# A two-layer diffusion transformer on one core: the conv border's weight parts, the place of modulation units, PSUM banks, one head's scaling and the last weight block

## The chip, the cores and the metric

The kernel runs on one core of a Trainium2 chip. The metric is the device time of one execution in microseconds (us), the median over runs. TensorE (PE) multiplies, VectorE (DVE), ScalarE (ACT) and GpSimd (POOL) work element by element, and SyncE (SP) issues the transfers from HBM. Each engine executes its own list of instructions in order and waits on semaphores for the others.

## The reference

The program computes two layers (D = 1024) on 256 latent and 256 context tokens, all in fp32. Layer 0 mixes with a short convolution, layer 1 with grouped-query attention over 8 heads. Both have a gated FFN (2816 hidden) before and after the mixer, and each of these three sub-blocks is normalised, modulated by vectors that depend on the condition, and gated:

```python
mod = (silu(c) @ mod_w[i] + mod_b[i]).reshape(bsz, 3, 3, 1, D_MODEL)
lat = lat + 0.5 * mod[:, 0, 2] * swiglu(modulate(lat, norm_g[i, 0], mod[:, 0, 0], mod[:, 0, 1]), w13[i, 0], w2[i, 0])
h = modulate(lat, norm_g[i, 1], mod[:, 1, 0], mod[:, 1, 1])
y = short_conv_mixer(h, ...)        # layer 0;  gqa_mixer(h, hc, ...) in layer 1
lat = lat + mod[:, 1, 2] * y
lat = lat + 0.5 * mod[:, 2, 2] * swiglu(modulate(lat, norm_g[i, 2], mod[:, 2, 0], mod[:, 2, 1]), w13[i, 1], w2[i, 1])
# modulate(t, g, shift, scale) = rms(t) * g * (1 + scale) + shift
```

The context goes the same way (with its own modulation) up to where layer 1's attention has read its keys and values. The result is the latent part.

## The kernel before, in words

**Precision.** [...] Every operand is split in a high part (`wh`, `hh`, ...: ScalarE copies) and a low part (`wl`, `hl`, ...: VectorE subtracts), and a product is three matmuls (`mm3`, L137 to L140), in some stages two. So each block of weights needs a transfer, a copy on ScalarE (1.0 us for 1024 columns) and a subtraction on VectorE (1.2 us) before TensorE can use it.

**Weights.** SP issues all weight transfers in one queue, into `wr` (two buffers of 1 MB); the split parts lie in `wh` and `wl`, four buffers of 1024 columns each. A matmul that is done with a part frees it for the next.

**Modulation.** The vectors `mod` are computed on VectorE by 224 *modulation units* (`mod_unit`, L157, output `junk`): each multiplies 128 rows of the transposed modulation weights with the condition and sums them. Their raw data comes through `wm` (two buffers of 512 KB, `mod_raw`), a transfer serving one or two units. Units are spread over the program by `tick(n)`: it adds n to an account, and for each whole 1 in it puts the next unit at this point of VectorE's order.

**Stages and borders.** The residual `x` is held as eight blocks of 128 columns. Between two stages stands a border: the last two blocks of a projection are finished (`fin`), squared, summed by small matmuls with a column of ones (`ss`, L256), the inverse root is spread over the rows (L276), and the scaled residual (`hr`, by `scaled`) is multiplied and split into the next stage's operands. `open_border` writes this order out by hand. `late(i, s)` are matmuls of the last two blocks that are kept back to give TensorE work meanwhile; `bd.nk` counts the blocks of the projection's inner dimension. With 8 of them the border is *short*: this is only the case from the conv mixer to layer 0's second FFN. `whi(i)` and `wlo(i)` split the first weight halves of the new stage; `ready()` is a square root of one column of the sum so far, on ScalarE.

**FFN.** `border_ffn` follows `open_border` into an FFN: three blocks (`pg`, `pu`) are multiplied plainly, and while that runs the operands and the first weights (`pr`) for block *pairs* are prepared: `Pair` multiplies 2 x 2 blocks with seven products in place of eight, from sums and differences of the weights that VectorE makes (`sub`, L762 to L769, `wr<-wr`; split parts at L744 and L747). From there `ffn` goes over the pairs, each of some 9.9 us, with `tick(PER_PAIR)`, 0.7 of a unit, in each.

**Attention.** PSUM banks are given out in pools by `use_banks`. Per head: `scores` (`psc`), `most` (maxima), `exps`, `weigh` (reciprocal of the sums, then `e` scaled in two halves of 512 on GpSimd, L1661), `turn` (transposes, `pt`, L1672), split, and `mix`.

**Last stage.** The last FFN's second product goes over the residual blocks m = 0 to 7. `w_last` fetches weights for two blocks at a time: two transfers `w2l` of 2048 columns, and `w2m` of 1536 columns, of which each block of the two uses 768, all through `wr`.

Inside borders, pairs and attention the order is the written one; elsewhere a scheduler orders by its own costs.

Of the kernel before, what the change touches and what calls it, by code (L numbers as in the profile page):

```python
# [16 lines left out]
P = 128  # L17
# [8 lines left out]
HEADS = 8  # L26
# [15 lines left out]
def hybrid_kernel(ctx: ExitStack, tc: tile.TileContext, a: dict, out: bass.AP):  # L42
# [29 lines left out]
    def psum(s="ps"):  # L72
        return banks["psm"].tile([P, T2], F32, tag="mm", name=nm(s))
# [36 lines left out]
    def mod_raw():  # L110
        return wp.tile([P, D], F32, name=nm("wm"), tag="wm", bufs=2)
# [5 lines left out]
    def half():  # L117

        return tuple(
            wp.tile([P, 1024], F32R, name=nm(t), tag=t, bufs=4) for t in ("wh", "wl")  # L120
        )
# [71 lines left out]
    def tick(n, behind=None):  # L193

        owed[0] += n
        while (jobs or units) and owed[0] >= 1:
            owed[0] -= 1
            if behind is None:
                next_unit()
            else:  # L200
                with tc.issue_after(behind.ins):
                    next_unit()
# [327 lines left out]
    def open_border(bd, v, early=False):  # L530


        short = bd.nk == KT
        mid = 5 if short else 6

        def whi(i):
            v[i][0].hi(v[i][1])

        def wlo(i):
            v[i][0].lo(v[i][1])  # L540

        ready()
        for s in range(2):
            for k in (4, 5):
                bd.scaled(k, s)
        bd.late(0, 0)
        if short:
            for i in range(2):
                whi(i)
                wlo(i)  # L550
        tick(2)
        bd.fin(0, 0)
        bd.square(0, 0)
        bd.late(0, 1)
        if not short:
            tick(1)
        bd.add(0)
        bd.fin(1, 0)
        bd.square(1, 0)
        bd.late(1, 0, range(mid))  # L560
        if not short:
            whi(0)
        bd.sums(0)
        bd.root(0)
        bd.late(1, 0, range(mid, bd.nk))
        bd.inv(0)
        bd.rows(0)
        if not short:
            wlo(0)
            whi(1)  # L570
        bd.fin(0, 1)
        bd.late(1, 1)
        bd.mult(0, 0)
        bd.square(0, 1)
        bd.hi(low, 0)
        if not short:
            wlo(1)
        bd.add(1)
        bd.mult(1, 0)
        if early:  # L580
            whi(2)
        bd.fin(1, 1)
        bd.hi((4, 5), 0)
        bd.square(1, 1)
        bd.hi((6, 7), 0)
        bd.lo(low, 0)
        return whi, wlo
# [17 lines left out]
    def ready():  # L605

        t = const.tile([P, 1], F32, name=nm("ready"), tag="ready")
        nc.scalar.activation(out=t, in_=accs[0][:, :1], func=AF.Sqrt)
# [216 lines left out]
    def border_ffn(l, b, h, bd):  # L825


        w = [Halves(a["w13"][l, b, i]) for i in range(2)]
        whi, wlo = open_border(bd, [(w[i], j) for i in range(2) for j in range(2)])
        w.append(Halves(a["w13"][l, b, 2]))  # L830
        gs = [new_pair("g") for _ in range(2)]
        pp = [(psum("pg"), psum("pu")) for _ in range(2)]
        post = [Post(p) for p in pp]
        for i in range(2):
            post[i].four(gs[i])

        def groups(i, s):
            return [
                (pp[i][j][:, s * S : s * S + S], lambda k, j=j: w[i]((1 - j) * 1024 + k * P))
                for j in range(2)  # L840
            ]

        def whole(i, s):
            for n in range(3):
                part_mm(groups(i, s), range(KT), n, s, h, True, True)

        g = groups(0, 0)
        for n in range(2):
            part_mm(g, low, n, 0, h, True, False)
        whi(2)  # L850
        bd.sums(1)
        bd.root(1)
        part_mm(g, low, 2, 0, h, False, False)
        bd.lo(high, 0)
        bd.inv(1)
        for n in range(2):
            part_mm(g, high, n, 0, h, False, False)
        whi(3)
        bd.rows(1)
        part_mm(g, high, 2, 0, h, False, True)  # L860
        wlo(2)
        wlo(3)
        pr = Pair(a["w13"][l, b, 3], h)
        bd.shift(low, 0)
        bd.mult(0, 1)
        bd.mult(1, 1)
        bd.shift(high, 0)
        whole(1, 0)
        bd.hi(low, 1)
        bd.lo(low, 1)  # L870
        bd.hi(high, 1)
        bd.lo(high, 1)
        whole(0, 1)
        bd.shift(low, 1)
        tick(1)
        bd.shift(high, 1)
        h.sub(0)
        h.hi("T1")
        h.sub(1)
        h.sub(2)  # L880
        h.lo("T1")
        h.hi("T2")
        post[0].silu()
        h.lo("T2")
        post[0].gate()
        whole(1, 1)
        for i in range(2):
            w[2].hi(i)
            w[2].lo(i)
        post[0].gh()  # L890
        h.sub(3)
        post[0].gl()
        h.hi("T3")
        h.lo("T3")
        pr.hi("A")
        post[1].silu()
        pr.hi("A22")
        pr.lo("A")
        post[1].gate()
        pr.lo("A22")  # L900
        post[1].gh()
        pr.sub(0)
        pr.sub(1)
        pr.hi("S12")
        pr.sub(2)
        post[1].gl()
        pp.append((psum("pg"), psum("pu")))
        for s in range(2):
            g = groups(2, s)
            for n in range(3):  # L910
                part_mm(g, low, n, s, h, s == 0, False)
        for k in high:
            for ps, at in ((pp[2][j], lambda k, j=j: w[2]((1 - j) * 1024 + k * P)) for j in range(2)):
                mm3(ps, at(k), pick(h, k, 0, T2), False, k == KT - 1, True)
        return gs, pr, Post(pp[2])

    def ffn(l, b, h, gate, norm, gs=(), ev=1.5, bd=None):
# [3 lines left out]
        for t in range(2):  # L921
            between = ()
            with tc.manual_schedule(engines=set(QUEUES[:3])) if bd else nullcontext():
# [29 lines left out]
                with nullcontext() if bd else tc.manual_schedule(engines=set(QUEUES[:3])):  # L953
                    for i in range(i1, n):
                        pr, nxt = pair(i), pair(i + 1)
                        if i > i1:
                            pr.lo("S12")
                            pr.lo("S34")
                        elif bd:
                            pr.lo("S12")  # L960
                            pr.hi("S34")
                            pr.lo("S34")
                        pair(i + 2)
                        ask_ahead()
                        if prev:
                            prev.silu()
                        pr.head()
                        if done:
                            done.gate()
                        if nxt:  # L970
                            nxt.both("A22")
                            nxt.sub(0)
                        if done:
                            done.gate_parts()
                        if bd and i == i1:
                            h.hi("T4")
                            h.lo("T4")
                        pr.five()
                        if prev:
                            tick(PER_PAIR)  # L980
                            prev.seven()
                        if nxt:
                            nxt.both("A")
                            nxt.sub(1)
                            nxt.sub(2)
                        pr.six()
                        if nxt:
                            nxt.hi("S12")
                            nxt.hi("S34")
                        if prev:  # L990
                            gs.append(new_pair("g"))
                            prev.four(gs[-1])
                        done, prev = prev, pr
# [661 lines left out]
    def weigh(hd):  # L1655
        e, sm = es[hd]
        r = ap.tile([P, 2], F32, name=nm("r"), tag="r", bufs=3)
        nc.vector.reciprocal(r, sm)
        for qt in range(2):
            c = slice(qt * T2, qt * T2 + T2)  # L1660
            nc.gpsimd.tensor_scalar(  # L1661
                out=e[:, c], in0=e[:, c], scalar1=r[:, qt : qt + 1], scalar2=None, op0=ALU.mult
            )

# [34 lines left out]
    with tc.manual_schedule(engines=set(QUEUES)):  # L1699
# [21 lines left out]
        lo_of(*wvc[1])  # L1721
        sq3 = squares(pq[3])
        g3 = gained(pq[3], qg, 2)
        use_banks(("psc", 2), ("ptp", 2), ("pav", 2))
        scores(0)
        scores(1)
        kc2 = by_cos(*g2)
# [285 lines left out]
    def w_last(m):  # L2013
        if m // 2 not in box:
            t = m // 2
            box[t] = (
                load_w(a["w2l"][t, 0]), load_w(a["w2l"][t, 1]), load_w(a["w2m"][t], 12 * P)
            )
        o = m % 2
        return lambda k: box[m // 2][o](k * P) if k < 16 else box[m // 2][2]((o * 6 + k - 16) * P)  # L2020

    for m in range(KT):
        w = w_last(m)
# [81 lines left out]
```

## Time and profile before

| | us |
|---|---|
| median of 3 runs (lowest to highest) | 1577.05 (1576.33 to 1577.66) |
| the profiled execution | 1575.96 |
| its span in the trace | 1573.9 |
| TensorE busy | 1557.0 (99%) |
| VectorE busy | 1286.5 (82%) |
| ScalarE busy | 755.2 (48%) |
| GpSimd busy | 34.2 (2%) |

Times in the trace count from the start of its span. Where the text says "chain of waits", it is the chain of work followed back from the last instruction, each step to what released it. In windows, the columns are the stretch, its length, the busy time of TensorE, its weight loads, VectorE, ScalarE and GpSimd (with numbers of instructions), the granted TensorE clock (1.00 is full), the busy share of the DMA engines and GB/s. The borders spoken of lie at 550 to 570 us (short, conv to FFN) and 913 us (layer 0 to layer 1); the first pairs behind them start at 613 and 963; attention's scores start at 1314, its head 7 is turned at 1353; the last stage runs from 1506.

### The profile page before, as it was taken

How to read it: one execution, taken by the hardware profiler on the slowest of the kernel's cores; microseconds unless marked ns; L12 is line 12 of the kernel's file. 1: busy time of each engine (PE TensorE's matmuls, PEld its weight loads, DVE VectorE, ACT ScalarE, POOL GpSimd, SP SyncE). 2: the span in 40 equal slices, each digit the busy share in tenths (PEclk: the TensorE clock that was granted, in tenths of full speed). 3: DMA queues.
4: the chain of work that ended last, by engine and by line, in shares of the span. 5: the costliest groups of instructions: out<-in, count | busy, mean ns of one | idle time of the engine just before them, and what ended most of it. 6: DMA issues, size and time to landing. Idle time of an engine off the chain costs nothing.

```text
span 1573.9 us, 25256 instructions
## 1 busy us (share of the span) xinstructions
PE 1557.0 (99%) x10240; PEld 1422.7 (90%) x10240; DVE 1286.5 (82%) x1905; ACT 755.2 (48%) x1261; POOL 34.2 (2%) x28
## 2 busy tenths in 40 slices
PE   9999999999999989999999999999999999999998
PEld 7789899989888889998999899988999899998887
DVE  5788879996999578996999878997998776776654
ACT  4524245535322365532554475532554465775542
POOL 0000000000000000000000000000000002320000
PEclk9999999999999999999999999999999999999999
DMA  9363633363566412355334523357335632345553
GB/s 360 131 209 130 205 111 131 105 212 132 196 214 199 136 67 99 130 188 162 120 122 146 202 95 121 126 197 240 125 131 194 211 124 87 108 161 193 192 176 136
DMA packets 51747, 248.75 MB, mean 158 GB/s; under 512 B 6704, under 2 KB 9264, under 8 KB 36400
## 3 DMA queue, kind: packets, MB, share of 16 engines
q1 hardware_dynamic: 50912, 246.98, 46.1%
q8 instruction: 80, 1.31, 0.3%
q14 instruction: 35, 0.29, 0.1%
q10 hardware_dynamic: 720, 0.17, 0.0%
HBM read 244.77 MB, written 1.05 MB: 156 GB/s over the span
## 4 chain that ended last, share of the span: by engine, by line
PE 94%; DVE 2%; ACT 1%; DMA 1%; issue 0%; POOL 0%; ACTq 0%; DVEq 0%; POOLq 0%
PE py L138 9%; PE py L140 9%; PE py L139 9%; PE p L138 6%; PE p L140 6%; PE p L139 6%; PE q L140 5%; PE q L138 4%; PE q L139 4%; PE pu L1817 3%; PE pg L1817 3%; PE py L1817 2%; PE pg L522 2%; PE pu L522 2%; PE pg L1202 1%; PE pv L138 1%
## 5 line engine op out<-in xcount | busy, mean ns | idle before, releaser
L114 ACT ACTIVATE wh<-wr 128x1024 fp32r<-128x1024 f32 (+1 forms) x210 | 190.7, 926 | 248.4 <-PE py L139 128.1
L157 DVE CUSTOM_DVE_ANT_0 junk<-wm,scbc,modb 128x1024 bf16<-128x1024 f32 x224 | 286.9, 1281 | 24.6 <-DMA wm<-in_modT 22.7
L115 DVE TENSOR_TENSOR wl<-wr,wh 128x1024 fp32r<-128x1024 f32 (+1 forms) x210 | 220.1, 1060 | 71.8 <-ACT wh L114 29.7
L138 PE MATMUL py<-gh,wh 128*128 128x512 f32 (+1 forms) x594 | 217.8, 367 | 0.0
L139 PE MATMUL py<-gl,wh 128*128 128x512 f32 (+1 forms) x594 | 217.3, 366 | 0.0
L140 PE MATMUL py<-gh,wl 128*128 128x512 f32 (+1 forms) x594 | 217.1, 365 | 0.0
L747 DVE TENSOR_TENSOR wl<-wr,wh 128x1024 fp32r<-128x1024 f32 x156 | 186.1, 1218 | 27.7 <-ACT wh L744 27.7
L744 ACT ACTIVATE wh<-wr 128x1024 fp32r<-128x1024 f32 x156 | 160.5, 1056 | 100.5 <-DVE wr L767 59.0
L140 PEld LDWEIGHTS py<-gh,wl 128*128 128x128 f32 x594 | 112.1, 189 | 17.9
L138 PEld LDWEIGHTS py<-gh,wh 128*128 128x128 f32 x594 | 112.1, 189 | 17.7
L139 PEld LDWEIGHTS py<-gl,wh 128*128 128x128 f32 x594 | 112.1, 189 | 17.6
L140 PE MATMUL p<-th,wl 128*128 128x256 f32 x416 | 117.7, 283 | 0.0
L139 PE MATMUL p<-tl,wh 128*128 128x256 f32 x416 | 117.7, 283 | 0.0
L138 PE MATMUL p<-th,wh 128*128 128x256 f32 x416 | 117.7, 283 | 0.0
L138 PE MATMUL q<-bh,wh 128*128 128x256 f32 x304 | 86.0, 283 | 0.0
L139 PE MATMUL q<-bl,wh 128*128 128x256 f32 x304 | 86.0, 283 | 0.0
L140 PE MATMUL q<-bh,wl 128*128 128x256 f32 x304 | 86.0, 283 | 0.0
L139 PEld LDWEIGHTS p<-tl,wh 128*128 128x128 f32 x416 | 79.8, 192 | 0.2
L138 PEld LDWEIGHTS p<-th,wh 128*128 128x128 f32 x416 | 79.8, 192 | 0.2
L140 PEld LDWEIGHTS p<-th,wl 128*128 128x128 f32 x416 | 79.8, 192 | 0.0
L762 DVE TENSOR_TENSOR wr<-wr 128x1024 f32<-128x1024 f32 x52 | 63.7, 1225 | 1.6
L114 ACT ACTIVATE gh<-gm 128x512 fp32r<-128x512 f32 x60 | 37.8, 631 | 52.1 <-DVE gm L820 47.7
(372 smaller groups left out, 4098.1 us busy)
## 6 DMA issues: line engine op xcount, KB each, us to landing
wr<-in_w SPq DMA_DIRECT2D x85, 1024.0 KB, 4.8
wm<-in_modT SPq DMA_DIRECT2D x128, 512.0 KB, 4.2
wr<-in_w2h SPq DMA_DIRECT2D x48, 704.0 KB, 5.3
mr<-in_mod SPq DMA_DIRECT2D x16, 512.0 KB, 8.5
wr<-in_cw_cx SPq DMA_DIRECT2D x8, 1024.0 KB, 4.8
wr<-in_w2l SPq DMA_DIRECT2D x8, 1024.0 KB, 4.9
wr<-in_cw_b SPq DMA_DIRECT2D x4, 1024.0 KB, 5.2
wr<-in_cw_out SPq DMA_DIRECT2D x4, 1024.0 KB, 5.7
```

The costliest lines, as they stand in the source:

```text
L114: nc.scalar.activation(out=hi, in_=src, func=AF.Copy)
L115: nc.vector.tensor_tensor(out=lo, in0=src, in1=hi.bitcast(F32), op=ALU.subtract)
L138: nc.tensor.matmul(ps, wh, mh, start=first, stop=False, **kw)
L139: nc.tensor.matmul(ps, wh, ml, start=False, stop=False, **kw)
L140: nc.tensor.matmul(ps, wl, mh, start=False, stop=last, **kw)
L157: nc.vector.tensor_tensor_reduce(out=junk, in0=raw, in1=scbc[:, v, :], scale=1.0, scalar=modb[:, l, col : col + 1], op0=ALU.mult, op1=ALU.add,
L522: nc.tensor.matmul(ps, w[n == 1], hl if n == 2 else hh, start=first and n == 0 and k == ks[0] and (first is True or g == 0), stop=last and ...
L744: nc.scalar.activation(out=self.shaped(g, 0), in_=self.part(g), func=AF.Copy)
L747: nc.vector.tensor_tensor(out=self.shaped(g, 1), in0=self.part(g), in1=self.shaped(g, 0).bitcast(F32), op=ALU.subtract,)
L762: tt(out=by_two(raw[:, :1024]), in0=a21.unsqueeze(1).to_broadcast([P, 2, T2]), in1=by_two(raw)[:, :, :T2], op=ALU.subtract,)
L1202: nc.tensor.matmul(pps[i][j], w[j][n == 1], hl if n == 2 else hh, start=k == 0 and n == 0, stop=k == KT - 1 and n == 2,)
L1817: nc.tensor.matmul(p[:, :n], w(j, k)[part], m(k)[:, :n], start=not part and k == 0, stop=part == 1 and k == nk - 1, skip_group_check=True,)
```

## The change

Five edits:

1. In the short border the first two weight halves are split (`whi`, `wlo`) ahead of `ready()` in place of behind the scaled residual, and of the two units there one goes behind `fin(1, 0)`.
2. In `border_ffn` two units are put behind `post[1].gl()`; the first pair behind a border gets none (0.7 before).
3. For attention the pools are placed in another order: transposes and outputs get the banks that scores had, scores the last four.
4. Head 7's `e` is scaled by VectorE in place of GpSimd.
5. `w_last` fetches `w2m` as two transfers of 768 columns through the `wm` buffers, each with a split of its own.

```diff
@@ open_border
+        if short:
+            for i in range(2):
+                whi(i)
+                wlo(i)
         ready()
         for s in range(2):
             for k in (4, 5):
                 bd.scaled(k, s)
         bd.late(0, 0)
-        if short:
-            for i in range(2):
-                whi(i)
-                wlo(i)
-        tick(2)
+        tick(1 if short else 2)
         bd.fin(0, 0)
...
         bd.fin(1, 0)
+        if short:
+            tick(1)
         bd.square(1, 0)
@@ border_ffn
         post[1].gl()
+        tick(2)
@@ ffn
                         if prev:
-                            tick(PER_PAIR)
+                            tick(0 if bd and i == i1 else PER_PAIR)
                             prev.seven()
@@ weigh
-            nc.gpsimd.tensor_scalar(
+            eng = nc.vector if hd == HEADS - 1 else nc.gpsimd
+            eng.tensor_scalar(
                 out=e[:, c], in0=e[:, c], scalar1=r[:, qt : qt + 1], scalar2=None, op0=ALU.mult
             )
@@ attention
-        use_banks(("psc", 2), ("ptp", 2), ("pav", 2))
+        use_banks(("ptp", 2), ("pav", 2), ("psc", 2))
@@ w_last
-            box[t] = (
-                load_w(a["w2l"][t, 0]), load_w(a["w2l"][t, 1]), load_w(a["w2m"][t], 12 * P)
-            )
+            ws = [load_w(a["w2l"][t, j]) for j in range(2)]
+            for j in range(2):
+                raw = mod_raw()[:, : 6 * P]
+                nc.sync.dma_start(raw, a["w2m"][t][:, j * 6 * P : (j + 1) * 6 * P])
+                ws.append(tuple(u[:, : 6 * P] for u in half()))
+                split(*ws[-1], raw)
+            box[t] = ws
```

ScalarE in the short border, before (`sq_5068` and `sq_5129` are the squares of residual blocks 4 and 5, `wr_5134` the new stage's first weights):

```order
346 L244 ACTIVATE sq_5068<-x 128x512
347 L244 ACTIVATE sq_5129<-x 128x512
348 L608 ACTIVATE ready_5138<-acc_4938 128x1
349 L412 ACTIVATE hr_5081<-x,A_5077 128x256 x2
350 L412 ACTIVATE hr_5083<-x,A_5077 128x256 x2
351 L498 ACTIVATE wh_5169<-wr_5134 128x1024
352 L498 ACTIVATE wh_5173<-wr_5134 128x1024
353 L437 ACTIVATE sq_5184<-x 128x256
```

And now:

```order
346 L244 ACTIVATE sq_5068<-x 128x512
347 L498 ACTIVATE wh_5138<-wr_5134 128x1024
348 L498 ACTIVATE wh_5142<-wr_5134 128x1024
349 L244 ACTIVATE sq_5129<-x 128x512
350 L610 ACTIVATE ready_5146<-acc_4938 128x1
351 L412 ACTIVATE hr_5081<-x,A_5077 128x256 x2
352 L412 ACTIVATE hr_5083<-x,A_5077 128x256 x2
353 L437 ACTIVATE sq_5180<-x 128x256
```

The two `wh` moved not only ahead of `ready` and `hr`, but ahead of the last whole square too.

VectorE at the same place, before (`py_5102` is block 5 of the projection, `py_5144` and `py_5187` are the late blocks 6 and 7 of the first half of the tokens):

```order
673 L594 TENSOR_SCALAR x<-py_5102,mod_5_3329,x 128x256 x2
674 L247 TENSOR_TENSOR acc_4938<-acc_4938,sq_5129 128x512
675 L503 TENSOR_TENSOR wl_5170<-wr_5134,wh_5169 128x1024
676 L503 TENSOR_TENSOR wl_5174<-wr_5134,wh_5173 128x1024
677 L157 ISA junk_5177,mod_0_4956<-wm_5039,scbc,modb 128x1024
678 L157 ISA mod_0_4956 128x1
679 L157 ISA junk_5179,mod_0_4956<-wm_5039,scbc,modb 128x1024
680 L157 ISA mod_0_4956 128x1
681 L429 TENSOR_SCALAR x<-py_5144,mod_5_3329,x 128x256
682 L442 TENSOR_TENSOR acc_4938<-acc_4938,sq_5184 128x256
683 L429 TENSOR_SCALAR x<-py_5187,mod_5_3329,x 128x256
```

And now:

```order
673 L503 TENSOR_TENSOR wl_5139<-wr_5134,wh_5138 128x1024
674 L596 TENSOR_SCALAR x<-py_5102,mod_5_3329,x 128x256 x2
675 L503 TENSOR_TENSOR wl_5143<-wr_5134,wh_5142 128x1024
676 L247 TENSOR_TENSOR acc_4938<-acc_4938,sq_5129 128x512
677 L157 ISA junk_5177,mod_0_4956<-wm_5039,scbc,modb 128x1024
678 L157 ISA mod_0_4956 128x1
679 L429 TENSOR_SCALAR x<-py_5152,mod_5_3329,x 128x256
680 L442 TENSOR_TENSOR acc_4938<-acc_4938,sq_5180 128x256
681 L429 TENSOR_SCALAR x<-py_5183,mod_5_3329,x 128x256
682 L157 ISA junk_5210,mod_0_4956<-wm_5039,scbc,modb 128x1024
683 L157 ISA mod_0_4956 128x1
```

The `wl` stand around the residual's block 5, and one unit in place of two is left ahead of the late blocks.

VectorE at the end of the border at 601 us, before (`gl_5312` is the last operand of the plain blocks, `wr_5388` the first pair's weights):

```order
720 L698 TENSOR_TENSOR gl_5312<-gm_5611,gh_5311 128x512
721 L747 TENSOR_TENSOR wl_5618<-wr_5388,wh_5617 128x1024
722 L747 TENSOR_TENSOR wl_5700<-wr_5388,wh_5699 128x1024
723 L747 TENSOR_TENSOR w4l_5736<-wr_5696,w4h_5735 128x512
724 L762 TENSOR_TENSOR wr_5696<-wr_5696 128x1024
```

And now:

```order
720 L700 TENSOR_TENSOR gl_5312<-gm_5611,gh_5311 128x512
721 L157 ISA junk_5622,mod_0_4956<-wm_5075,scbc,modb 128x1024
722 L157 ISA mod_0_4956 128x1
723 L157 ISA junk_5626,mod_0_4956<-wm_5212,scbc,modb 128x1024
724 L157 ISA mod_0_4956 128x1
725 L749 TENSOR_TENSOR wl_5618<-wr_5388,wh_5617 128x1024
726 L749 TENSOR_TENSOR wl_5706<-wr_5388,wh_5705 128x1024
```

Two units now stand ahead of the pair's first split parts.

More of the change, by code (lines that the diff above doesn't have):

```diff
@@ L2015, in w_last, with at @@
             t = m // 2
-            box[t] = (
-                load_w(a["w2l"][t, 0]), load_w(a["w2l"][t, 1]), load_w(a["w2m"][t], 12 * P)
-            )
-        o = m % 2
-        return lambda k: box[m // 2][o](k * P) if k < 16 else box[m // 2][2]((o * 6 + k - 16) * P)
+            ws = [load_w(a["w2l"][t, j]) for j in range(2)]
[5 more added lines that the diff above has]
+            box[t] = ws
+        o = m % 2
+        ws = box[m // 2]
+        def at(k):
+            if k < 16:
+                return ws[o](k * P)
+            return tuple(u[:, (k - 16) * P : (k - 15) * P] for u in ws[2 + o])
+        return at
     for m in range(KT):
```

## The prediction

> **What bounds the kernel now.** I read the page first: its busy row, then the shares of the chain that ended last.
>
> ```profile
> span 1573.9 us, 25256 instructions
> PE 1557.0 (99%) x10240; PEld 1422.7 (90%) x10240; DVE 1286.5 (82%) x1905; ACT 755.2 (48%) x1261; POOL 34.2 (2%) x28
> PE 94%; DVE 2%; ACT 1%; DMA 1%; issue 0%; POOL 0%; ACTq 0%; DVEq 0%; POOLq 0%
> ```
>
> TensorE has work for 1557.0 of 1573.9 us and carries 94% of the chain. The change leaves the number of matmuls as it is, so all it can win is time in which TensorE waits, or runs below its clock. The second view is therefore the list of waits of TensorE (who waited for whom: us in total, times, longest).
>
> ```profile
> PE ss L256 <- DVE acc L442: 3.9, 1, 3.9
> PE ss L1129 <- DVE sq L1125: 1.7, 1, 1.7
> PE psc L138 <- ACT kn L1447: 1.3, 1, 1.3
> PE pt L1672 <- POOL e L1661: 1.2, 2, 0.9
> PE p L140 <- DVE wl L747: 0.9, 2, 0.5
> PE py L1817 <- ACT wh L114: 0.4, 2, 0.2
> PE ss L256 <- ACT sq L437: 0.3, 1, 0.3
> ```
>
> Five of these rows belong to the places that the change edits; L1129 (the start of the program) does not. The largest is one wait of 3.9 us, in the border from the conv stage to the second FFN of layer 0. Third view: the stretches around it (length, PE busy, PEld, DVE, ACT, POOL, granted clock, DMA share, GB/s).
>
> ```profile
> 557.85:561.74 3.89, 0.01 (x1) 0.00 (x0) 3.37 (x7) 0.81 (x2) 0.00 (x0) 0.85 0.72 251
> 561.74:567.41 5.67, 5.41 (x24) 5.33 (x25) 1.35 (x4) 1.77 (x5) 0.00 (x0) 0.50 0.30 105
> 567.41:570.11 2.70, 2.70 (x25) 2.70 (x24) 2.33 (x3) 1.93 (x6) 0.00 (x0) 1.00 0.00 0
> ```
>
> TensorE stands for 3.89 us, and then runs 5.67 us at clock 0.50. The wait costs more than its length. Fourth view: the chain of waits through that place (start, us, what).
>
> ```profile
> 550.35 0.89 DVE x L594 x2
> 551.32 0.64 ACT sq L244
> 551.98 0.70 DVE acc L247
> 552.81 1.69 ACT hr L412 x4
> 554.51 0.96 ACT wh L498
> 555.49 2.36 DVE wl L503 x2
> 557.85 1.20 DVE junk L157
> 559.09 1.28 DVE junk L157
> 560.38 0.41 DVE x L429
> 560.82 0.42 ACT sq L437
> 561.26 0.42 DVE acc L442
> ...
> 562.59 1.44 PE ss L256 x6
> ...
> 570.11 0.48 PE pg L522 x4
> ```
>
> It reads: after the last square, ScalarE does four `hr` and only then the two `wh`; VectorE, in order, waits for them, does two `wl` and two modulation units (`junk`), and only at 560.38 the residual `x` whose square the sums need.
>
> **The change, part by part.**
>
> *A, the short border.* The two `wh` and `wl` now stand ahead of `ready`, and one of the two units goes behind `fin(1, 0)`. I replay the chain with its own durations. The weight data lies in SBUF in time (before, `wh` waits for nothing but the `hr` ahead of it). Buffers: `wl` and `wh` of the last conv block are freed by TensorE's matmuls of that block, the second pair with its end, where the chain's 550.35 starts. So the first pair is done by then, and `wh(1)` runs 550.45 to 551.5 beside the two `x`; queued behind it on ScalarE is only the square, 0.1 to 0.2 us late (552.1). `wl(1)` follows to 552.7, `acc` to 553.4, one unit to 554.6, `x` of fin(0,0) to 555.0; ScalarE is through its four `hr` at about 555.2, squares to 555.6; `acc` to 556.05, `x` of fin(1,0) to 556.5, its square to 556.95. TensorE arrives at 557.7 or 557.85, and 0.7 to 0.9 us of margin remain. So the 3.89 us and the 0.26 us before 562.59 go, and with them the half clock. What is left from 557.85 to 570.11 (12.26 us) is 2.70 us of work at full clock and 5.41 us at half, which is 2.70 at full: 5.40. Gain 6.86; and the first `ss` starts some 0.15 us before 557.85, where the modelled end of the last matmul is. I take **7.0**. Next late would be the operands of `pg`: from the sums to `pg` VectorE has 1.35 and 2.33 us of work in the last two windows, ScalarE 1.77 and 1.93, so 3.7 us each, partly one after the other, which must now fit into 5.4 us; I cost it at nothing, with a wait of up to 0.3 us in the range.
>
> That the clock fell with the wait I read from the row. [...]
>
> *B, the two FFN borders (after conv, and from layer 0 to layer 1).* Two units now stand behind `post[1].gl()`, and the first block pair has none.
>
> ```profile
> 602.70:606.00 3.30, 3.30 (x18) 2.79 (x17) 0.12 (x2) 1.11 (x2) 0.00 (x0) 1.00 0.00 0
> 612.86:622.75 9.89, 9.38 (x74) 8.80 (x73) 9.79 (x14) 5.54 (x9) 0.00 (x0) 1.00 0.47 159
> 622.75:632.60 9.85, 9.85 (x84) 9.85 (x84) 9.71 (x13) 5.54 (x9) 0.00 (x0) 1.00 0.32 109
> ```
>
> The first pair (second row) gets 74 matmuls done in 9.89 us, the next 84 in 9.85, with VectorE 9.79 us busy: the pair waits for VectorE. At the next pair's 0.117 us a matmul, 74 are 8.68: 1.2 us are lost, and the other border's first pair (at 963) looks alike. The units are 2 x 1.28 = 2.56 us. Their new place is a stretch in which VectorE does 0.12 us in 3.30 (first row), so they fit with 0.6 us to spare; the `wl` behind them would end at 605.3, and TensorE wants it at 605.9. Removing 1.28 us ahead of the first pair's `wl` covers the 1.2. I take **2.4** for both. With the units the next modulation transfer moves ahead on SP's queue, past one weight transfer (the third pair's); that one waits for a buffer of its own, which the first pair frees, so I cost this at nothing, and at most the some 4 us of a transfer, hidden behind a pair of 9.9, if it is held up. If that cover is gone, `wl` comes up to 2.56 us late.
>
> *C, the banks.* Scores get the last four PSUM banks in place of those of the last projection, so the first score no longer waits 1.3 us for `kn` to read one. But VectorE's row of maxima and sums behind the scores is full and stays where it was; the first transpose waits for it instead. Bounds: 0 to 1.5; nearest to what stays, I take **0.35**.
>
> *D, head 7.*
>
> ```profile
> L1661 POOL TENSOR_SCALAR e<-e,r x9: 1562/1563/1570, 1338.9 to 1353.7; 128x512 f32<-128x512 f32 x9
> L1375 DVE TENSOR_SCALAR d<-u,convk x8: 477/481/487, 405.1 to 515.5; 128x512 f32<-128x512 f32 x8
> ```
>
> Two operations of 1.56 us leave GpSimd; on VectorE the same form takes 0.48, together 0.96. The scaled head is ready 2.2 us earlier, but TensorE waited 1.2 for it, and the copies of head 6 (`ptl`) queue 0.96 us later on VectorE behind it. Bounds 0.2 and 1.2; I take **0.75**. [...]
>
> *E, the last stage.* One row of four columns a block pair:
>
> ```profile
> 1506.26:1521.71 15.45, 15.45 (x90) 13.44 (x89) 7.93 (x12) 7.64 (x12) 0.00 (x0) 1.00 0.49 176
> 1521.71:1537.76 16.05, 15.81 (x90) 13.38 (x89) 8.15 (x11) 4.45 (x6) 0.00 (x0) 1.00 0.58 197
> 1537.76:1553.61 15.85, 15.79 (x91) 13.37 (x89) 8.19 (x11) 6.43 (x9) 0.00 (x0) 1.00 0.61 200
> 1553.61:1569.50 15.89, 15.69 (x89) 13.25 (x88) 6.70 (x9) 4.16 (x6) 0.00 (x0) 1.00 0.19 66
> ```
>
> The first pair of rows takes 15.45 us; the three others, which wait for the third weight transfer and its `wh`, 0.60, 0.40 and 0.44 more: 1.44. Through the modulation buffers, free by then, that transfer is asked for about 10 us ahead. The number of splits is the same (two of 768 columns for one of 1024 and one of 512). I take **1.3**. The first two halves are asked for before the last loads of layer 1's first FFN, behind its last units; at no cost, as those loads wait for their own buffer longer.
>
> Where the scheduler works, a few `py` matmuls and a unit change places in the FFN's projects: 0, with 1 us either way.
>
> **Sum:** 7.0 + 2.4 + 0.35 + 0.75 + 1.3 = 11.8 us. The profiled execution took 1575.96 us (span 1573.9 and 2.06 around it), so 1564.2 for its like; the median of the runs, 1577.05, lies 1.1 above it: **1565.3**. About 0.2%, 3.2 us, is what a measurement of this kernel can tell from no change.
>
> **Rivals.**
>
> 1. *The border's wait is shortened, not gone.* A square queued behind `wh(1)`, or `pg`'s operands, come late. For: the replay's margin is 0.7 us over six handovers between ScalarE and VectorE. With a wait as long as the second one of the list, 1.7 us, A is 5.3 and the time 1567.0; with A all lost, 1572.3. [...]
>
> 2. *VectorE gives B, C and D back.* It is 9.7 of 9.85 us busy in the FFN pairs and queued without a break in attention: what TensorE no longer waits for there, it waits for one step later. Only A and E stay, 8.3: 1568.8.
>
> 3. *All covers hold and C and D give their upper bounds*: 7.0 + 2.4 + 1.5 + 1.2 + 1.44 = 13.5: 1563.5.
>
> 4. *Slower: the two moved units wait for their data* in the FFN borders, with `wl` behind them on VectorE and TensorE behind that.
>
> ```profile
> DVE junk L157 <- DMA wm<-in_modT: 22.7, 22, 3.3
> ```
>
> Units have waited up to 3.3 us for a transfer. If they do so in both new places, TensorE stands about 3.3 us, and if the clock halves as in the short border another 2.85 (7.0 less 3.89 and 0.26): 6.2 a border, 12.3 in all, and B's 2.4 isn't won. 9.4 less 12.3 is 2.9 lost: 1580.0. It decides where both waits are about 3 us; against it, the buffers that the two units read are filled from transfers that stand ahead of the first pair's weights on SP's queue, and 22 waits that come to 22.7 us are 1.0 us each on average.
>
> **Chances:** forecast 0.60, rival 1 0.16, rival 2 0.09, rival 3 0.06, rival 4 0.06, and 0.03 that parts fail on top of a lost A so that nothing is to be seen. The forecast's own bounds are about 2 us either way (project order 1, D 0.5, C and `pg` 0.3 each). The range goes from 1562.5, past rival 3, to 1571, which takes in most of rivals 1 and 2. Faster by over 0.2%: 0.91; within: 0.03; slower: 0.06.
>
> **What would show it.** A: no row `ss L256 <- acc` among TensorE's waits, granted clock 1.00 throughout 555 to 570, `pg` at about 563. B: the first pairs with about 84 matmuls in 9.85 us, and `wl` ahead of them not late. C: `psc` no longer waits for `kn`, `pt` waits a little more. D: no `pt <- POOL e` for head 7, but some `pt` or `po` after `ptl`. E: four periods of about 15.5 us. It would be wrong if the clock row still shows 0.50 at 561, or if a new wait of over 1.5 us stands in TensorE's list behind a `junk` or an `hr`.

## The result, and the profile after

The changed kernel takes 1564.09 us (median of 4 runs, 1563.47 to 1564.38), the kernel before 1577.05: a ratio of 0.9917, 95% interval 0.9900 to 0.9935. In a second series it was 1562.34 against 1576.5, ratio 0.9909 (0.9896 to 0.9923). The forecast was 1565.3.

The page of the changed kernel, its span, busy row and chain by engine:

```profile
span 1562.1 us, 25254 instructions
PE 1553.3 (99%) x10240; PEld 1421.4 (91%) x10240; DVE 1287.5 (82%) x1907; ACT 755.4 (48%) x1261; POOL 31.1 (2%) x26
PE 97%; DVE 1%; ACT 0%; DMA 0%; issue 0%; POOL 0%; ACTq 0%; DVEq 0%; POOLq 0%
```

The span is 11.8 us shorter. The same 10240 matmuls keep TensorE busy 3.7 us less, although none was removed. 2.7 of this is, by my estimate, the half clock of the short border: 5.41 us of matmuls at 0.50, taken as half of that at 1.00. (In the changed kernel's trace, matmuls of 512 columns start every 0.43 us at 0.50, from 22.00 to 24.56, and every 0.23 us at 1.00, from 25.30 to 25.76.) The first pairs, the FFN project at 1214 and the last stage have 2.3 less, since the profile models a matmul's end and counts part of a short wait as busy (9.38 us for the first pair's 74 matmuls before, 8.99 now); the start of the program, which no edit touches, has 1.4 more. All rows of its list of waits:

```profile
PE pt L1676 <- POOL e L1665: 1.3, 2, 1.0
PE ss L1132 <- DVE sq L1128: 1.3, 1, 1.3
PE idle L1054 <- DVE eps_t L96: 1.1, 1, 1.1
PE pg L1205 <- ACT hh L1189: 0.8, 1, 0.8
PE pt L1676 <- DVE ptl L1542: 0.3, 1, 0.3
```

The border's 3.9 us are gone, as are `psc`, `p L140` and `py`. What is left is the start of the program, and the transposes, `pt`: 1.05 us for GpSimd at the first one, which is new, 0.30 at head 6 as before, and 0.27 for `ptl` at head 7. Through the short border, stretches and chain:

```profile
556.00:558.20 2.20, 2.20 (x22) 2.20 (x20) 1.74 (x4) 0.82 (x3) 0.00 (x0) 1.00 0.40 164
558.20:563.57 5.37, 5.37 (x48) 5.37 (x47) 3.30 (x6) 2.67 (x7) 0.00 (x0) 1.00 0.30 98
```

```profile
558.28 0.79 PE ss L256 x8
...
560.24 0.44 PE ss L276 x4
563.57 0.56 PE pg L522 x4
```

TensorE doesn't stop, the granted clock stays 1.00, and `pg` starts at 563.57 instead of 570.11. The first pair, and the four periods of the last stage:

```profile
606.39:615.38 8.99, 8.99 (x74) 8.74 (x73) 8.92 (x13) 5.54 (x9) 0.00 (x0) 1.00 0.31 117
1496.22:1511.66 15.44, 15.44 (x90) 13.54 (x89) 9.28 (x13) 7.63 (x12) 0.00 (x0) 1.00 0.46 165
1511.66:1527.06 15.40, 15.40 (x90) 13.44 (x89) 8.11 (x11) 6.66 (x8) 0.00 (x0) 1.00 0.60 205
1527.06:1542.47 15.41, 15.41 (x89) 13.45 (x89) 8.12 (x11) 6.66 (x8) 0.00 (x0) 1.00 0.61 205
1542.47:1557.84 15.37, 15.37 (x90) 13.41 (x88) 5.65 (x8) 2.44 (x4) 0.00 (x0) 1.00 0.05 17
```

The first pair does its 74 matmuls in 8.99 us without a pause (9.89 before); all four periods take 15.4 us.

To place the gain I compare when the same matmul, by its number in TensorE's order, starts in two traces. A step in this difference is what was won at that place; what lies ahead of the place drops out. Differences to the kernel before, in us:

| place | changed kernel, step | forecast |
|---|---|---|
| start of the program (same code) | +0.60 | - |
| FFN project at 327 (same code) | -0.24 | - |
| short border (A) | -6.89 | -7.0 |
| first pairs at 613 and 963 (B) | -0.90, -1.11 | -2.4 |
| FFN project at 1214 | -0.59 | 0 |
| first score, then first transpose (C) | -1.59, +1.26 | -0.35 |
| head 7 (D) | -0.81 | -0.75 |
| last stage (E) | -1.48 | -1.3 |

With 0.1 us of small steps between them they come to 11.7. The steps at the start and at 327 are not of the change: up to 547 us TensorE, VectorE, ScalarE and GpSimd have the same work in the same order in both kernels, and over all traces of this study the first lies between -0.6 and +1.2 us, the second between -0.27 and +0.15.

### The profile page after: what moved, and what is told of

The parts are those of the page before. It is cut to its first block, busy times and chain, and to the rows that moved or that the text cites. A ratio compares the mean times of both kernels' runs of the same rounds, so it can differ in the third digit from the quotient of the medians.

```text
span 1562.1 us, 25254 instructions
## 1 busy us (share of the span) xinstructions
PE 1553.3 (99%) x10240; PEld 1421.4 (91%) x10240; DVE 1287.5 (82%) x1907; ACT 755.4 (48%) x1261; POOL 31.1 (2%) x26
## 3 DMA queue, kind: packets, MB, share of 16 engines
HBM read 244.77 MB, written 1.05 MB: 157 GB/s over the span
## 4 chain that ended last, share of the span: by engine, by line
PE 97%; DVE 1%; ACT 0%; DMA 0%; issue 0%; POOL 0%; ACTq 0%; DVEq 0%; POOLq 0%
PE py L138 9%; PE py L139 9%; PE py L140 9%; PE p L138 6%; PE p L140 6%; PE p L139 6%; PE q L140 5%; PE q L138 5%; PE q L139 5%; PE py L1821 4%; PE pu L1821 3%; PE pg L1821 3%; PE pg L522 2%; PE pu L522 2%; PE pg L1205 1%; PE pu L1205 1%
## 5 line engine op out<-in xcount | busy, mean ns | idle before, releaser
L114 ACT ACTIVATE wh<-wr 128x1024 fp32r<-128x1024 f32 (+1 forms) x202 | 184.4, 929 | 243.5 <-PE py L139 120.5
L115 DVE TENSOR_TENSOR wl<-wr,wh 128x1024 fp32r<-128x1024 f32 (+1 forms) x202 | 212.9, 1064 | 57.9 <-ACT wh L114 25.4
L138 PE MATMUL py<-gh,wh 128*128 128x512 f32 (+1 forms) x594 | 217.8, 367 | 0.0
L140 PE MATMUL py<-gh,wl 128*128 128x512 f32 (+1 forms) x594 | 217.1, 365 | 0.0
L140 PEld LDWEIGHTS py<-gh,wl 128*128 128x128 f32 x594 | 112.0, 189 | 18.1
L138 PEld LDWEIGHTS py<-gh,wh 128*128 128x128 f32 x594 | 112.1, 189 | 17.7
L140 PE MATMUL p<-th,wl 128*128 128x256 f32 x416 | 117.7, 283 | 0.0
L138 PE MATMUL p<-th,wh 128*128 128x256 f32 x416 | 117.7, 283 | 0.0
L138 PE MATMUL q<-bh,wh 128*128 128x256 f32 x304 | 86.0, 283 | 0.0
L140 PE MATMUL q<-bh,wl 128*128 128x256 f32 x304 | 86.0, 283 | 0.0
L138 PEld LDWEIGHTS p<-th,wh 128*128 128x128 f32 x416 | 79.8, 192 | 0.2
L140 PEld LDWEIGHTS p<-th,wl 128*128 128x128 f32 x416 | 79.8, 192 | 0.0
```

Of the source, the lines that this page charges most:

```text
L114: nc.scalar.activation(out=hi, in_=src, func=AF.Copy)
L115: nc.vector.tensor_tensor(out=lo, in0=src, in1=hi.bitcast(F32), op=ALU.subtract)
L138: nc.tensor.matmul(ps, wh, mh, start=first, stop=False, **kw)
L140: nc.tensor.matmul(ps, wl, mh, start=False, stop=last, **kw)
```

## Experiments

**A, the two edits apart.** Only the unit is moved behind `fin(1, 0)`:

```diff
-        tick(2)
+        tick(1 if short else 2)
         bd.fin(0, 0)
...
         bd.fin(1, 0)
+        if short:
+            tick(1)
         bd.square(1, 0)
```

> The kernel before, with one thing of part A alone: of the two units in the short border one goes behind fin(1, 0); wh and wl stay where they were. The sums come one unit, 1.28 us, earlier, so TensorE's wait shrinks from 3.89 to about 2.6 us. [...] Rival (every wait of this size halves the clock, or the clock hangs on something else there): clock 0.50 again for about 5 us, gain 1.3 us, time about 1575.8.

1574.87 us against 1576.05, ratio 0.9992 (0.9983 to 1.0001); the step at the border is 0.64 us. Its waits, and stretches of 3.41 us, the first of which holds the wait:

```profile
PE ss L256 <- DVE acc L442: 2.6, 1, 2.6
```

```profile
557.61:561.02 3.41, 0.85 (x6) 0.56 (x5) 2.93 (x7) 0.82 (x3) 0.00 (x0) 1.00 0.55 168
561.02:564.43 3.41, 2.95 (x15) 2.95 (x15) 1.33 (x3) 1.07 (x3) 0.00 (x0) 0.50 0.62 215
564.43:567.85 3.42, 3.42 (x18) 3.42 (x18) 2.39 (x4) 1.47 (x4) 0.00 (x0) 0.50 0.19 78
```

The wait is 1.3 us shorter (2.56 for 3.89), as expected, but the clock still falls to 0.50, for 6.83 us as in the kernel before (560.58 to 567.41 there). I had taken it to stay at 1.00, for a gain of 4.1 us by my estimate (1.28 for the unit, 2.85 for the clock); the rival stood on the clock. Of the rival's 1.3 us only 0.64 arrives: the half-clock stretches now hold 6.37 us of matmuls (2.95 and 3.42) where the kernel before has 5.41, which by estimate costs 0.48 (half of the 0.96 more), and the second wait, for `sq`, is 0.46 where it was 0.26. The wait of 2.56 us was seen in one trace.

Only `wh` and `wl` are moved ahead of `ready()`, both units stay in front:

```diff
+        if short:
+            for i in range(2):
+                whi(i)
+                wlo(i)
         ready()
...
-        if short:
-            for i in range(2):
-                whi(i)
-                wlo(i)
         tick(2)
```

> The kernel before, with the other thing of part A alone: wh and wl of the first two weight halves ahead of ready; both units stay ahead of fin(0, 0). Theory: moving wh and wl carries nearly all; the chain of the sums is 1.28 us later than in the changed kernel, whose margin was 0.8 us, so TensorE waits 0 to 0.6 us, at full clock; gain 6.3 to 6.9 us, time about 1570.5. Rival (both edits of A are needed): a wait of over 1.3 us, gain under 5.5.

1569.19 us, ratio 0.9958 (0.9943 to 0.9973); the step at the border is 6.89 us, to the hundredth that of the whole part A, and TensorE doesn't wait:

```profile
556.00:558.20 2.20, 2.20 (x21) 2.20 (x21) 0.83 (x3) 1.64 (x4) 0.00 (x0) 1.00 0.88 326
558.20:562.00 3.80, 3.80 (x34) 3.80 (x34) 2.26 (x5) 1.48 (x4) 0.00 (x0) 1.00 0.11 44
```

So moving the weight parts is all of A. The unit behind `fin(1, 0)` adds nothing to it.

**The changed kernel without A.**

> The changed kernel with part A undone (wh and wl behind the scaled residual, both units ahead of fin(0, 0)). Theory: the parts add up, A is 6.9 us of the gain: the 3.9 us wait and the half clock are back, time about 1571.0. Rival (the parts share a cause, or the waits of one come back in another): 1566 to 1568, or over 1573.

1570.61 us, ratio 0.9965 (0.9952 to 0.9977). The wait is back at 3.9 us, the clock at 0.50, and the step at the border is 0.1 us in place of 6.9; all the other steps are those of the changed kernel within 0.2. The parts add up.

**How long a wait the clock bears.** Three units ahead of `fin(0, 0)` in the changed kernel:

```diff
-        tick(1 if short else 2)
+        tick(3 if short else 2)
```

> The changed kernel with three units in place of one ahead of fin(0, 0) in the short border. The changed kernel's margin at the sums was 0.8 us, two more units are 2.56 us, so TensorE waits about 1.7 us there. Theory (a wait well under 2.6 us leaves the clock alone): granted clock 1.00, the border costs 1.7 us more than in the changed kernel, of which units saved later give some back. Rival (any wait of over a microsecond there halves the clock): 1.7 + 2.8 = 4.5 us.

```profile
558.39:559.64 1.25, 0.38 (x3) 0.30 (x3) 1.25 (x3) 0.76 (x3) 0.00 (x0) 1.00 0.63 246
559.64:565.00 5.36, 5.36 (x45) 5.36 (x46) 3.99 (x7) 3.05 (x9) 0.00 (x0) 1.00 0.30 99
```

```profile
PE ss L256 <- ACT sq L437: 0.5, 1, 0.5
PE ss L256 <- DVE acc L442: 0.4, 1, 0.4
```

The two waits, 0.41 us for `acc` and then 0.46 for `sq`, each from the modelled end of the matmul ahead, cost 1.29 us at the border (step 5.60 for 6.89); the clock stays at 1.00. By the starts of the matmuls, which follow each other here every 0.12 us, some 0.6 us are lost at each. That is 0.4 us less than expected, since two units alone still fit under TensorE's work, as `a_wh_only` showed. The wait of 2.56 us in `a_split_only`, with the 0.46 behind it, cost 6.25 (step 0.64 for 6.89); no run has one between these lengths in this border.

**B, the two edits apart.** No unit in the first pair, none added in the border:

```diff
-                            tick(PER_PAIR)
+                            tick(0 if bd and i == i1 else PER_PAIR)
```

> The kernel before, with one thing of part B alone: no unit in the first pair behind an FFN border (0 for 0.7), no units added in the border. Theory (the unit ahead of the first pair's wl made the stall): both first pairs lose their stall, 0.9 and 1.1 us by the start times of the same matmul, 2.0 in all, and the units that are put off cost nothing. Rival (the units must go somewhere, and VectorE is full in the pairs): the stall turns up in the next pairs or in the next border, gain under 0.7.

1573.51 us (one run). Steps of 0.90 and 1.12 us at the first pairs, all of B, and 0.59 us more at the project at 1214, as in the changed kernel. The next pair does not pay:

```profile
612.70:621.70 9.00, 9.00 (x75) 8.76 (x74) 8.93 (x13) 5.54 (x9) 0.00 (x0) 1.00 0.34 117
621.70:631.50 9.80, 9.80 (x83) 9.80 (x84) 9.70 (x14) 5.54 (x9) 0.00 (x0) 1.00 0.49 163
```

The other half alone:

```diff
         post[1].gl()
+        tick(2)
```

> The kernel before, with the other thing of part B alone: two units behind post[1].gl() in the FFN border, the first pair keeps its 0.7. Theory (only taking the unit out of the first pair pays; the two in the border fill idle time): the first pairs keep their stall if they still hold a unit, gain 0 to 0.3 us by the start times of the same matmul at 621 and 978. Rival (the border's units are what pays, since later units come earlier): 0.9 and 1.1 us as in the changed kernel.

1577.81 us (one run): the steps at both first pairs are 0.0, and the pair is the old one:

```profile
614.40:624.35 9.95, 9.43 (x74) 8.85 (x74) 9.85 (x14) 5.54 (x9) 0.00 (x0) 1.00 0.50 158
```

So the two units in the border are neither the gain nor its price; they only keep the count. This run is 0.6 us slower at the short border, which it does not edit: there the half clock came later,

```profile
562.95:569.78 6.83, 6.43 (x31) 6.34 (x31) 2.52 (x6) 2.35 (x7) 0.00 (x0) 0.50 0.23 86
```

and 31 matmuls fell into it, where the kernel before had 24 in its 0.50 row.

**C undone in the changed kernel.**

> The changed kernel with part C undone (the pools in the old order). Theory: the first score waits 1.3 us for kn again, and the wait for GpSimd at the first transpose, 1.2 us in the changed kernel, shrinks by about as much, since the reciprocal of head 0's sums comes at the same time; from the first score to head 7 the kernel is 0.3 us slower, and head 7's gain is untouched. Rival (the banks are worth the whole wait): 1.6 us slower with the transpose's wait as it is.

1564.52 us (one run). The steps at the first score and the first transpose are 0.0 and 0.0, for 1.59 and minus 1.26 in the changed kernel. Its two rows:

```profile
PE psc L138 <- ACT kn L1450: 1.3, 1, 1.3
...
PE pt L1676 <- POOL e L1665: 0.3, 1, 0.3
```

The banks took away a wait of 1.3 us and a new one of 1.0 at the first transpose took its place: 0.33 us net, as forecast.

**Who took C back.** In the changed kernel VectorE's reciprocal of head 0's sums stands behind a `wl` of 1.22 us that nobody needs yet. One line moved:

```diff
         turned(*g3, kc3)
-        lo_of(*woc[0])
...
         weigh(0)
+        lo_of(*woc[0])
```

> The changed kernel with one line moved: VectorE's wl of the output projection's first weights (1.22 us) behind the reciprocal of head 0's sums in place of ahead of it. The sums are there at 1312.50, VectorE is through kn at 1313.18 and then does wl until 1314.32; GpSimd's first half of e, 1.56 us, ends at 1316.14 and TensorE waits for it from 1314.98 to 1316.19. Theory (this wl holds the chain that took back part C's gain): the reciprocal comes 1.1 us earlier, the wait falls to 0.1 us, gain 1.1 us. Rival (VectorE's row is full, so the next step, vl or the maxima, takes it back): gain under 0.4 us.

1562.88 us, ratio 0.9917 (0.9901 to 0.9934). The reciprocal came as early as expected, the transpose did not: the step there improves by 0.33 us and not by 1.1. The chain of waits shows why:

```profile
1312.35 0.09 DVE r L1661
...
1312.61 2.37 POOL e L1665
...
1315.03 0.66 PE pt L1676 x4
```

GpSimd took 2.37 us for what takes 1.57 in the changed kernel (the median of its 14 scalings is 1.56 in this run too). In VectorE's order the moved `wl`, 1.20 us, stands there behind the reciprocal. Neither my theory nor the rival had this: the row of VectorE was free, but GpSimd was 0.80 us slower. Why, no run shows.

Scaling the first half of head 0's `e` on VectorE avoids GpSimd for the half that TensorE waits for:

```diff
-            eng = nc.vector if hd == HEADS - 1 else nc.gpsimd
+            eng = nc.vector if hd == HEADS - 1 or (hd, qt) == (0, 0) else nc.gpsimd
```

> The changed kernel with the first half of head 0's e scaled by VectorE too, 0.48 in place of 1.56 us. Theory: the first transpose starts 1.0 us earlier, all behind it on VectorE 0.45 us later; by the start times of the same matmul 0.6 to 1.0 us faster behind the first transpose, some of it given back by the maxima of head 2. Rival (VectorE is the bound there): 0 to 0.3.

1563.47 us (one run). The first transpose has no wait, the step there is -1.55 us in sum, 1.24 better than the changed kernel, and nothing is given back up to the end. It was then timed:

> The changed kernel with the first half of head 0's e on VectorE, timed. By its trace it gains 1.23 us behind the first transpose. Theory: time 1.2 us below the changed kernel in the same series, near what such a series can tell, if at all. Rival (something behind the transpose gives it back in most executions): no difference.

> The changed kernel itself, in the same series as the version with head 0's half on VectorE, to be compared with it: 1564.1 as before, 0.8% below the kernel before.

1561.50 us (1560.98 to 1563.06) against 1562.34 (1561.62 to 1563.88) for the changed kernel in the same series. The times point the right way by 0.8 us, but overlap; the gain rests on the traces, in which it came twice (1.24 and 1.22 us).

**D and E undone.**

> The changed kernel with parts D and E undone (head 7 on GpSimd, w2m as one transfer through wr). Theory: by the start times of the same matmul, head 7's turn costs 0.8 us more again, and the last stage 1.5 us more, in three waits for wh at 0.2 to 0.4 us; nothing else moves: 2.3 us in all. Rival (what D and E won came from elsewhere, from units and the scheduler's order): under 1.2 us.

1567.03 us (one run). At head 7 the step is 0.0 for 0.81, in the last stage plus 0.1 for minus 1.5: 2.4 us in all, as expected. Head 7 waits for GpSimd again:

```profile
1342.93 3.12 POOL e L1665 x2
1346.05 0.04 issue
1346.09 0.44 PE pt L1676 x2
```

## Why the prediction was right

**A.** The mechanism held: 7.0 was forecast, 6.9 came. The replay put `x` of fin(1,0) to end at 556.5, its square at 556.95, and TensorE's arrival 0.7 to 0.9 us later; the trace, 0.4 us later from the start on, has 557.00, 557.46 and 558.28. That this agrees nearly to the tenth is luck, since two errors cancel. The `acc` ahead of this `x` ends at 556.06, 0.4 us earlier than replayed when the late start is taken off, and then VectorE stands 0.46 us for TensorE's late block, a wait that the replay doesn't have:

```profile
556.52 0.48 DVE L429 SCALAR_TENSOR_TENSOR x<-py,mod,x 128x256 f32<-128x256 f32 x1 [0.46 <-PE py L140]
```

What I had wrong was which edit does it: the unit put behind `fin(1, 0)` is not needed (left in front, it fills this wait, and `a_wh_only` has none there), and alone it yields 0.64 us. Rival 1's 1567.0 takes a wait of 1.7 us at its length alone, with the clock at 1.00. No run shows that in this border: there the clock stayed at 1.00 with the 0.41 and 0.46 us of `units3`, and was at 0.50 behind the 2.56 us of `a_split_only`. With the latter A would have been 0.64 in place of 7.0 and the time 1571.7.

**B.** The mechanism held, the size was off: 2.0 for 2.4. The term was taken from matmuls per us in two windows; by start times the stall was 0.9 and 1.1, since the first pair's 74 matmuls take 8.99 us without a wait and not 8.68. The two units in the border are free, as said, but they do not help either.

**C and D** came near their terms, 0.33 for 0.35 and 0.81 for 0.75. A wait further on took most of C, as said; its size was a choice between 0 and 1.5, so that it hit is luck. VectorE's 0.48 us against 1.56 decided D (the two moved halves took 0.48 each). But its upper bound was misread: the 1.2 us for GpSimd in the list are two waits, 0.88 at head 7 and 0.30 at head 6, and the second is still there.

**E** is 0.2 us larger than the 1.3 taken, that is, the whole 1.44 of the three longer periods. The traces show the early request as the cause: for the period from 1521.71 the kernel before asked for `w2m` at 1522.68, and ScalarE stood 4.86 us until it landed; the changed kernel asks at 1503.32 for the period from 1511.66, 8.3 us ahead. What the smaller splits do without it was not tried.

**Sum.** 11.8 was forecast; 12.96 came by the medians, 14.2 in the second series. By the traces it is 11.7, with 0.6 lost at the start and 0.24 won at 327, where no edit is, so 12.1 for the edits; the second trace of the changed kernel gives 12.1 too. What the medians have above this is not explained; single times of the kernel before run from 1574.0 to 1578.0. Of the 0.3 between 12.1 and 11.8, the project at 1214 gave 0.6 that I had put at 0 with 1 either way (it comes with the units taken from the first pair, as `b_pair_only` shows; a wait `p L138 <- DVE p L811` of 0.33 us goes there, whose row the prediction's list does not show), E 0.2, B minus 0.4. So errors of both signs cancel, and the closeness of the sum is in part luck. Rivals 2 and 4 didn't occur: in the pairs VectorE does not give the time back, and no unit waited for its data there. Of the seven waits that the prediction shows, six and not five belong to the edited places.

## What to carry to other kernels

Look for what stands in front of a chain on an in-order engine without being needed by it: here two copies of weights that were in SBUF long before, and behind them a residual on which all waited. Judge a wait of TensorE by what the clock does after it: in the short border two waits of 0.4 and 0.5 us cost 1.3 together, one of 2.6 us cost about 6, one of 3.9 us cost 7, so shortening a long wait may bring little where removing it brings everything. And compare two traces by the start of the same matmul: it told parts of 0.3 us apart where the times of runs scatter by 1 to 3. Its limit is what places without an edit move from trace to trace, here up to 0.45 us (the project at 1214 in `a_wh_only`), so a small step is safe only when it comes in several traces.

## What the runs showed of the hardware

**The granted clock.** In the kernel before it was at 0.50 from 11.04 to 17.86 and from 560.58 to 567.41 (6.82 and 6.83 us), and at 1.00 in the 542.72 us between. In the changed kernel it was at 0.50 from 11.50 to 18.32 and from 21.74 to 25.15 (6.82 and 3.41 us), all at the start of the program, and at 1.00 in the short border. In `a_split_only` it was at 0.50 from 561.02 to 567.85; in the 3.41 us ahead TensorE was busy for 0.85, with a wait of 2.56. In `b_border_only`, with a wait of 3.9 us, it was at 0.50 from 562.95 to 569.78. In `units3`, with waits of 0.41 and 0.46 us, it was 1.00 from 556.00 to 565.00.

Shorter waits than 2.56 us stand ahead of a half clock at the start of the program: 1.67 us in the kernel before and 1.28 in the changed kernel, each followed by sums of a single column (`ss`, 128x1). In the kernel before TensorE was busy for 2.53 us in the 3.42 ahead of 11.04, in the changed kernel for 3.17 in the 3.41 ahead of 11.50. The wait of 1.3 us ahead of the first score in the kernel before left the clock at 1.00, as it was from 567.41 to 1573.90. So the length of a wait alone does not sort these cases; what does, the runs don't show.

**GpSimd beside VectorE.** In `weigh_first` one of GpSimd's 14 scalings of 128x512 took 2.37 us, where the median is 1.56; VectorE had the moved `wl` (128x1024, 1.20 us) there. In the changed kernel all 14 took 1.56 to 1.57, also the first, which starts at 1314.58 while VectorE does `vl` (0.40 us from 1314.31) and goes on to another `vl` and `ql` (0.40 us from 1314.70, 0.69 from 1315.13). In `head0_half` the three from 1314 to 1321 took 1.63 us on average. The scaling of 2.37 us was seen once, in one run.
